# Softmax times values: the values' loads and the ordinary stores move from SyncE's queue to ScalarE's

## The chip, the cores and the metric

The kernel runs on one core of a Trainium2 chip. The metric is the device time in microseconds, the median over several runs. The core's engines are TensorE (PE, with weight loads as PEld), VectorE (DVE), ScalarE (ACT), GpSimd (POOL) and SyncE (SP), which here only issues transfers. A transfer that an engine issues goes into that engine's DMA queue, and 16 DMA engines carry it out.

## The reference

```python
# scores: (8, 12, 1024, 1024) float32, v: (8, 12, 1024, 64) float32
scores_max = np.max(scores, axis=-1, keepdims=True)
attn = np.exp(scores - scores_max)
attn = attn / (np.sum(attn, axis=-1, keepdims=True) + 1e-8)
return np.matmul(attn, v).astype(np.float32)
```

There are 96 heads. Scores are 402.7 MB, values and output 25.2 MB each, so 453 MB cross between HBM and the core's memory.

## The kernel before

The heads are taken four at a time in 24 passes (PASSES), in a hardware loop over m. A pass has two halves, k = 0 and k = 1, of two heads each. Each half has one score buffer s_bufs[k] of 128 partitions by 16 rows (R) by 1024 numbers: a partition holds 16 consecutive rows of one head, 64 KB, and one load(k, m) fills the buffer with 8.39 MB.

For each pair of rows ScalarE takes the exponential into half precision (L425; no maximum is subtracted, and a check at the end of the program turns to a slow general version if numbers leave a safe range). PE transposes (L438), VectorE copies the transposed block out of PSUM (L450, single rows at the end of a pass at L446), and PE multiplies by the values with two columns of ones beside them, which gives the sums of the rows (L160). The product of a row comes three rows (LAG) behind its transposes. VectorE divides (L139, L147) into out_bufs.

The values of a pass, 1.05 MB, are loaded into one tile, v_sb (load_v, L271), in the middle of the pass before. From there POOL spreads them as half precision into vones: spread_v(0) when the last product of k = 0 is done, spread_v(1) at the end of the pass (L283). ScalarE reads them too: watch_v (L295) at the end of a pass checks their range. At the end of a pass POOL also copies the outputs into the tile done (put_by, L178), which is stored in the middle of the next pass by store_before (L191). The last passes differ: the loads for the last two passes come in parts, the outputs of pass 21 wait in done and those of pass 22 in the place of the values (spare), and these and the last pass's own outputs go out through store_last (L202).

All transfers of the loop are issued by SyncE, in an order that is written out: queue(dma) makes each one follow the one before it on that engine. In the middle of pass m load_first (an If at L254) issues the values of pass n = m + 1, the store, and load(0, n); at the end of the pass last (an If at L384, with one at L388 inside) issues load(1, n). A load waits until the exponentials have read the buffer, so load(0, n) waits for the exponentials of k = 0 in pass m. Every load and store of the loop uses one of eight semaphores in turn. Where the two branches of an If use different ones, SyncE makes up for those of the branch not taken at the end of the If, and waits for the transfer that used each of them last.

Of the kernel before, what the change touches and what calls it, by code (L numbers as in the profile page):

```python
# [26 lines left out]
def kernel(  # L27
# [6 lines left out]
    nc = tc.nc  # L34
    P = 128
# [18 lines left out]
    K = AHEAD // T  # L54
    W = P // T
    R = SQ // W
    PASSES = BH // AHEAD
# [2 lines left out]
    GROUPS = -(-R // G)  # L60

    sc_rows = scores.rearrange("b h (j r) k -> (b h j) r k", j=W).rearrange(
        "(m x) r k -> m x r k", x=P
    )
    v_bh = v.rearrange("b h (i t) d -> (b h i) (t d)", i=Q)
    out_rows = out.rearrange("b h (j r) d -> (b h j) (r d)", j=W)
# [21 lines left out]
    done = sb_pool.tile([P, K, R * D], FP32, name="done")  # L88
# [11 lines left out]
    spare = v_sb[:].rearrange("x h s l d -> x (h s l d)").rearrange("x (k y) -> x k y", k=K)  # L100
# [8 lines left out]
    queued = []  # L109
    line = []  # L110

    def after(a, b):

        tc.add_manual_dep(
            a.ins,
            b.ins.name,
            mybir.DependencyInfo(mybir.DependencyClass.NoSync, mybir.DependencyReason.DATA),
            reason="order",
        )
# [7 lines left out]
    def queue(dma):  # L127

        if queued:
            after(dma, queued[-1])  # L130
        queued.append(dma)
# [42 lines left out]
    def put_by(homes):  # L174

        for k in range(K):
            fills.append(
                nc.gpsimd.tensor_copy(  # L178
                    out=homes[:, k], in_=out_bufs[k][:].rearrange("x r d -> x (r d)")
                )  # L180
            )

    def of_pass(m):

        rows = out_rows.rearrange("(m k x) y -> m x k y", k=K, x=P)
        return rows[bass.ds(m, 1)].rearrange("o x k y -> (o x) k y")

    def store_before(m):

        before = (m + (PASSES - 1)) % PASSES  # L190
        send(nc.sync.dma_start(out=of_pass(before), in_=done[:], cond=(before < PASSES - 3)))  # L191

    def send(dma):
        for other in stores:
            apart(dma, other)
            apart(other, dma)
        apart(dma, dma)
        stores.append(dma)
        queue(dma)

    def store_last(to, rows):
        store = nc.sync.dma_start(out=to, in_=rows)  # L202
        ends.append(store)
        send(store)

    def end():

        cut = (GROUPS - 2) * G
        for k, a, b in ((0, 0, R), (1, 0, cut), (1, cut, R)):
            n = BH - AHEAD + T * k  # L210
            store_last(
                out_rows[n * W : (n + T) * W, a * D : b * D],
                out_bufs[k][:, a:b, :].rearrange("x r d -> x (r d)"),
            )
# [4 lines left out]
    def apart(a, b, reason="stores of two heads are disjoint"):  # L219
        tc.declare_no_dep(a.ins, b.ins, across_iterations=True, reason=reason)  # L220
# [16 lines left out]
        users.setdefault((tile.name, bank), []).append(op)  # L237

    def load(k, m, parts=(R,), r=0, **cond):
        rows_n = sc_rows[bass.ds(m * K + k, 1)].rearrange("o x r k -> (o x) r k")  # L240
        for rows in parts:
            queue(
                nc.sync.dma_start(
                    out=s_bufs[k][:, r : r + rows, :], in_=rows_n[:, r : r + rows, :], **cond
                )
            )
            r += rows

    def load_first(m):


        before = queued[-1:]
        n = (m + 1) % PASSES
        with tc.If(m < PASSES - 1) as cmp:  # L254
            load_v(n)
            store_before(m)
            then = queued[-1:]
            with tc.If(m < PASSES - 3) as cmp2:  # L258
                load(0, n)
            with cmp2.Else():  # L260
                queued[:] = then
                load(0, n, (8, 4, 4))
        with cmp.Else():
            queued[:] = before
            store_last(of_pass(PASSES - 3), done[:])
            store_last(of_pass(PASSES - 2), spare)

    def load_v(m, **cond):

        rows = v_bh.rearrange("(m x) y -> m x y", x=P)  # L270
        dma = nc.sync.dma_start(  # L271
            out=v_sb[:].rearrange("x h s l d -> x (h s l d)"),
            in_=rows[bass.ds(m, 1)].rearrange("o x y -> (o x) y"),
            **cond,
        )
        fills.append(dma)
        queue(dma)

    def spread_v(k):

        for t in range(T):
            for s in range(S):
                op = nc.gpsimd.tensor_copy(  # L283
                    out=vones[s * Q : (s + 1) * Q, k, :, t, 0:D].rearrange(
                        "i (h l) d -> i h l d", l=L
                    ),
                    in_=v_sb[(k * T + t) * Q : (k * T + t + 1) * Q, :, s],
                )
        return op

    def watch_v():


        junk = p_bufs[-1][:].rearrange("p r k -> p (r k)")
        return nc.scalar.activation(  # L295
            out=junk,
            in_=v_sb[:].rearrange("p h s l d -> p (h s l d)"),
            func=mybir.ActivationFunctionType.Abs,
            scale=1.0 / SUM_MAX,
            accum_out=seen[:, K * R + 1 : K * R + 2],  # L300
        )
# [8 lines left out]
    def fold():  # L310

        n = K * R + 1
        nc.vector.tensor_reduce(out=seen[:, 0:1], in_=seen[:, 0 : n + 1], axis=X, op=ALU.min)  # L313
        nc.vector.tensor_reduce(  # L314
            out=seen[:, n + 1 : n + 2], in_=seen[:, 1 : n + 2], axis=X, op=ALU.max
        )

    def judge(bank):

        n = K * R + 1  # L320
        part = small("part")
        nc.vector.tensor_scalar(
            out=part, in0=seen[:, n + 1 : n + 2], scalar1=1.0, scalar2=None, op0=ALU.is_le
        )
        nc.vector.scalar_tensor_tensor(  # L325
            out=right, in0=seen[:, 0:1], scalar=1.0 / SUM_MAX, in1=part, op0=ALU.is_ge, op1=ALU.mult
        )
        cell = bank[0:1, G * M : G * M + 1]
        in_line(
            nc.tensor.matmul(  # L330
                out=cell, lhsT=right[:], rhs=vones[:, 0, 0, 0, D : D + 1], start=True, stop=True
            )
        )
        nc.vector.tensor_copy(out=count[:], in_=cell)  # L334
# [45 lines left out]
    def last(m, bank):  # L380

        before = queued[-1:]
        k = K - 1
        with tc.If(m < PASSES - 1) as cmp:  # L384
            spread = spread_v(k)
            watch = watch_v()
            n = (m + 1) % PASSES
            with tc.If(m < PASSES - 3) as cmp2:  # L388
                put_by(done)
                queued[:] = before  # L390
                load(k, n)
            with cmp2.Else():
                with tc.If(m < PASSES - 2) as cmp3:
                    put_by(done)
                with cmp3.Else():
                    gate = nc.gpsimd.tensor_copy(out=cell, in_=out_bufs[k][:, R - 1, D - 1 : D])
                    for op in (watch, spread):
                        tc.add_manual_dep(
                            gate.ins,
                            op.ins.name,  # L400
                            mybir.DependencyInfo(
                                mybir.DependencyClass.Sync, mybir.DependencyReason.DATA
                            ),
                            reason="the values have been read",
                        )
                    put_by(spare)
                queued[:] = before
                load(k, n, (4, 4, 2, 2, 2, 1, 1))
        with cmp.Else():
            queued[:] = before  # L410
            end()
            fold()
            judge(bank)

    def heads(m):

        for k in range(K):
            st = dict(psO=[take(psO_bufs) for g in range(GROUPS)])
            for r in range(R):
# [32 lines left out]
                if r == R - 1 and k < K - 1:  # L452
                    load_first(m)
# [3 lines left out]
        while pending:  # L457
            finish(pending.pop(0))
        last(m, st["psO"][-1])
        for store in ends:  # L460
            for fill in fills:
                apart(fill, store, "no pass comes behind the last stores")

    assert BH % AHEAD == 0 and BH >= 3 * AHEAD and SK == Q * S * C and K == 2
    load_v(0)
    for k in range(K):
        load(k, 0, (R // 2, R // 2) if k == 0 else (R,))
# [44 lines left out]
```

## Time and profile before

| | |
|---|---|
| time, median of 3 runs | 1059.47 us (1059.06 to 1059.63) |
| the profiled execution's own time | 1059.14 us |
| its span in the profile | 1057.4 us |
| mean granted clock of TensorE | 0.89 |
| DMA packets, bytes, mean rate | 19508, 453.06 MB, 428 GB/s |

The profile shows one execution. Busy shares are of the span. In rows of a timeline the first number is the start, the second the length of the stretch, both in us, and a bracket gives the idle time of the engine ahead of it and what ended that. SPq and ACTq are the queues of instructions of SyncE and ScalarE. In rows of DMA queues the columns are packets, MB and the time of the packets as a share of 16 engines over the window. In rows of stages the last three columns are the granted clock, the share of the DMA engines and GB/s.

### The profile page before, as it was taken

The numbers are of one execution on the slowest core, as the hardware profiler recorded it, in microseconds if no ns is written. First come the engines' busy times: TensorE is split into PE (matmuls) and PEld (weight loads), VectorE is DVE, ScalarE is ACT, GpSimd is POOL, SyncE is SP. The second block draws the span as 40 slices with busy tenths as digits, with TensorE's granted clock in tenths as the row PEclk, the third lists the DMA queues.
The fourth block names the chain that finished last, engine by engine and source line by source line (L and its number), as shares of the span: only waits on it lengthen the run. The fifth ranks groups of instructions, "written<-read, shape, count | busy, mean of one in ns | idle before, by whom it ended". The sixth has DMA issues, their size and how long they took to land. (4 is left out here: it accounts for less than half of the span.)

```text
span 1057.4 us, 32323 instructions
## 1 busy us (share of the span) xinstructions
PE 814.7 (77%) x12289; PEld 779.7 (74%) x12289; DVE 705.6 (67%) x1352; ACT 749.6 (71%) x482; POOL 285.5 (27%) x447
## 2 busy tenths in 40 slices
PE   3488678886787868877678877787787876878987
PEld 3487568786787767877668776787777866868887
DVE  2377566675676856767566675676656766667878
ACT  4487578776787667876778667786687856878965
POOL 3041231312412124122241221412224123231241
PEclk9799887898898988889888898898888988988999
DMA  9999999999999999999999999999999999999998
GB/s 397 438 437 421 410 455 426 429 429 425 448 436 436 436 430 440 424 434 431 424 434 434 436 436 436 436 434 414 449 431 434 424 424 441 436 436 420 431 421 322
DMA packets 19508, 453.06 MB, mean 428 GB/s; under 512 B 1840, under 2 KB 1968, under 8 KB 8624
## 3 DMA queue, kind: packets, MB, share of 16 engines
q1 hardware_dynamic: 19504, 452.99, 99.6%
q8 instruction: 4, 0.07, 0.0%
HBM read 427.82 MB, written 27.26 MB: 430 GB/s over the span
## 5 line engine op out<-in xcount | busy, mean ns | idle before, releaser
L425 ACT ACTIVATE p_nat<-s_nat 128x2048 f16<-128x2048 f32 (+1 forms) x432 | 702.4, 1709 | 291.7 <-SPq L388 153.1
L438 PE MATMUL psT<-ident,p_nat 128*128 128x128 f16 x6144 | 521.7, 236 | 213.7 <-ACT p_nat L425 212.3
L450 DVE COPY pt<-psT 128x2048 f16<-128x2048 f16 x336 | 411.3, 1224 | 310.0 <-PE L438 145.0
L438 PEld LDWEIGHTS <-p_nat 128*128 128x128 f16 x6144 | 436.9, 120 | 228.2 <-ACT p_nat L425 224.2
L160 PE MATMUL psO<-vones,pt 128*128 128x130 f16 x6144 | 499.4, 227 | 23.6 <-DVE pt L446 10.8
L283 POOL CAST vones<-v_sb 32x512 f16<-32x512 f32 x392 | 238.1, 607 | 763.6 <-PE L438 388.7
L160 PEld LDWEIGHTS <-pt 128*128 128x128 f16 x6144 | 400.9, 101 | 43.8 <-DVE pt L450 24.9
L147 DVE TENSOR_TENSOR out_sb<-psO,seen 64x192 f32<-64x192 f32 (+1 forms) x576 | 192.0, 333 | 22.1
L446 DVE COPY pt<-psT 128x1024 f16<-128x1024 f16 x96 | 63.4, 681 | 1.5
L139 DVE RECIPROCAL seen<-psO 128x3 f32<-128x3 f32 (+1 forms) x288 | 49.7, 172 | 12.3 <-PE L438 7.1
L295 ACT ACTIVATE p_nat<-v_sb 128x2048 f16<-128x2048 f32 x24 | 45.6, 1900 | 0.7 <-DMA v_sb<-in_v_dram 0.7
L178 POOL COPY done<-out_sb 128x1024 f32<-128x1024 f32 x44 | 44.4, 1035 | 4.7 <-issue 4.7
L295 ACT ACT_TABLE_LOAD x1 | 1.3, 1283 | 5.8 <-DMA v_sb<-in_v_dram 5.8
L313 DVE TENSOR_REDUCE seen<-seen 128x1 f32<-128x34 f32 x25 | 4.7, 189 | 0.8
L295 ACT ACTIVATION_READ_ACCUMULATOR p_nat<-v_sb 128x1 f32 x24 | 4.5, 188 | 0.0
L314 DVE TENSOR_REDUCE seen<-seen 128x1 f32<-128x34 f32 x25 | 4.5, 178 | 0.0
L97 DVE MEMSET done<- 128x1024 f32 x2 | 1.8, 912 | 1.2 <-DVEq L471 1.0
L178 POOL COPY v_sb<-out_sb 128x1024 f32<-128x1024 f32 x2 | 2.0, 1040 | 0.0
L330 PE MATMUL psO<-vones,right 128*1 128x1 f16 x1 | 0.2, 164 | 1.6 <-DVE right L325 1.6
L330 PEld LDWEIGHTS <-right 128*1 128x1 f16 x1 | 0.1, 79 | 1.8 <-DVE right L325 1.8
L334 DVE CAST count<-psO 1x1 int32<-1x1 f32 x1 | 0.1, 145 | 0.3 <-PE psO L330 0.3
masks.py:199 POOL TENSOR_SCALAR_AFFINE_SELECT ident<-ident 128x128 f32<-128x128 f32 x1 | 0.3, 292 | 0.1
(12 smaller groups left out, 1.7 us busy)
## 6 DMA issues: line engine op xcount, KB each, us to landing
v_sb<-in_v_dram SPq DMA_DIRECT2D x24, 1024.0 KB, 17.0
out_dram<-done SPq DMA_DIRECT2D x24, 1024.0 KB, 8.7
s_nat<-in_scores_dram SPq DMA_DIRECT2D x4, 4096.0 KB, 18.7
s_nat<-in_scores_dram SPq DMA_DIRECT2D x8, 2048.0 KB, 25.9
s_nat<-in_scores_dram SPq DMA_DIRECT2D x6, 1024.0 KB, 29.1
s_nat<-in_scores_dram SPq DMA_DIRECT2D x4, 512.0 KB, 26.8
out_dram<-v_sb SPq DMA_DIRECT2D x1, 1024.0 KB
s_nat<-in_scores_dram SPq DMA_DIRECT2D x43, 28.7
```

Of the source, the lines that this page charges most:

```text
L139: nc.vector.reciprocal(out=recip, in_=psO[:, :, D : D + 1])
L147: norm = nc.vector.tensor_tensor(out=out_bufs[k][part, g * G : g * G + rows, :], in0=psO[part, :, t * N : t * N + D], in1=recip[part].to_b ...
L160: product = nc.tensor.matmul(out=st["psO"][g][:, i * M : (i + 1) * M], lhsT=pt[:, c * P : (c + 1) * P], rhs=vones[:, k, c].rearrange("p t ...
L178: nc.gpsimd.tensor_copy(out=homes[:, k], in_=out_bufs[k][:].rearrange("x r d -> x (r d)"))
L283: op = nc.gpsimd.tensor_copy(out=vones[s * Q : (s + 1) * Q, k, :, t, 0:D].rearrange("i (h l) d -> i h l d", l=L), in_=v_sb[(k * T + t) * Q ...
L295: return nc.scalar.activation(out=junk, in_=v_sb[:].rearrange("p h s l d -> p (h s l d)"), func=mybir.ActivationFunctionType.Abs, scale=1. ...
L313: nc.vector.tensor_reduce(out=seen[:, 0:1], in_=seen[:, 0 : n + 1], axis=X, op=ALU.min)
L314: nc.vector.tensor_reduce(out=seen[:, n + 1 : n + 2], in_=seen[:, 1 : n + 2], axis=X, op=ALU.max)
L425: exp = nc.scalar.activation(out=p_nat[:, g : g + rows, :].rearrange("p r (x v) -> p x r v", v=Q * L), in_=s_bufs[k][:, r + g : r + g + ro ...
L438: turned = nc.tensor.transpose(out=psT[:, c * P : (c + 1) * P], in_=p_row[:, c // L, c % L, :], identity=ident16[:],)
L446: copy = nc.vector.tensor_copy(out=pt, in_=psT)
L450: copy = nc.vector.tensor_copy(out=pt2[:], in_=psT2[:])
```

## The change

The values' loads and the ordinary stores (those of passes 0 to 20) are issued by ScalarE; in the middle of a pass the store comes first, then the values. They are no longer in the order that queue keeps for SyncE. The two stores of passes 21 and 22 move from the middle of the last pass to its end, ahead of the last pass's own three, so that SyncE issues the last five stores together. In the last two passes the parts of load(0, n) are 4, 4, 4 and 4 rows instead of 8, 4 and 4, and those of load(1, n) are 4, 2, 2, 2, 2, 2, 1 and 1 instead of 4, 4, 2, 2, 2, 1 and 1. The scores are addressed by (m, k) instead of by m * K + k; the bytes are the same.

```diff
     sc_rows = scores.rearrange("b h (j r) k -> (b h j) r k", j=W).rearrange(
-        "(m x) r k -> m x r k", x=P
+        "(m g x) r k -> m g x r k", g=K, x=P
     )
...
     def store_before(m):
 
         before = (m + (PASSES - 1)) % PASSES
-        send(nc.sync.dma_start(out=of_pass(before), in_=done[:], cond=(before < PASSES - 3)))
+        send(nc.scalar.dma_start(out=of_pass(before), in_=done[:], cond=(before < PASSES - 3)))
...
         stores.append(dma)
-        queue(dma)
 
     def store_last(to, rows):
         store = nc.sync.dma_start(out=to, in_=rows)
         ends.append(store)
         send(store)
+        queue(store)
...
-        rows_n = sc_rows[bass.ds(m * K + k, 1)].rearrange("o x r k -> (o x) r k")
+        rows_n = sc_rows[bass.ds(m, 1), k].rearrange("o x r k -> (o x) r k")
...
         n = (m + 1) % PASSES
-        with tc.If(m < PASSES - 1) as cmp:
+        with tc.If(m < PASSES - 1):
+            store_before(m)
             load_v(n)
-            store_before(m)
-            then = queued[-1:]
             with tc.If(m < PASSES - 3) as cmp2:
                 load(0, n)
             with cmp2.Else():
-                queued[:] = then
-                load(0, n, (8, 4, 4))
-        with cmp.Else():
-            queued[:] = before
-            store_last(of_pass(PASSES - 3), done[:])
-            store_last(of_pass(PASSES - 2), spare)
+                queued[:] = before
+                load(0, n, (4, 4, 4, 4))
 
     def load_v(m, **cond):
 
         rows = v_bh.rearrange("(m x) y -> m x y", x=P)
-        dma = nc.sync.dma_start(
+        dma = nc.scalar.dma_start(
             out=v_sb[:].rearrange("x h s l d -> x (h s l d)"),
...
         fills.append(dma)
-        queue(dma)
...
                 queued[:] = before
-                load(k, n, (4, 4, 2, 2, 2, 1, 1))
+                load(k, n, (4, 2, 2, 2, 2, 2, 1, 1))
         with cmp.Else():
             queued[:] = before
+            store_last(of_pass(PASSES - 3), done[:])
+            store_last(of_pass(PASSES - 2), spare)
             end()
```

## The prediction

> **What bounds the kernel now.** I read the page first: the span, the busy shares, the DMA rows and the queues.
>
> ```profile
> span 1057.4 us, 32323 instructions
> PE 814.7 (77%) x12289; PEld 779.7 (74%) x12289; DVE 705.6 (67%) x1352; ACT 749.6 (71%) x482; POOL 285.5 (27%) x447
> ...
> DMA  9999999999999999999999999999999999999998
> ...
> q1 hardware_dynamic: 19504, 452.99, 99.6%
> ```
>
> No engine is above 77%, but the 16 DMA engines are full in every slice, and all of it is one queue, q1, SyncE's. Then the busy time by stage:
>
> ```profile
> 100.00:940.00 840.00, 655.00 (x9838) 627.11 (x9835) 564.33 (x1082) 595.79 (x385) 226.32 (x348) 0.88 1.00 433
> ```
>
> In the steady part the transfers run at 433 GB/s with a DMA share of 1.00. 452.99 MB at 433 GB/s are 1046 us of the 1057.4. So nothing that frees an engine can help there: the most that any change can win is about 11 us at the two ends, and a change loses wherever it lets the transfers stop. The timelines of SyncE's queue and of ScalarE show a steady pass:
>
> ```profile
> 423.51 0.33 SPq L271 DMA_DIRECT2D v_sb<-in_v_dram  x1
> 424.39 0.41 SPq L191 DMA_DIRECT2D out_dram<-done  x1
> 432.39 19.82 SPq L243 DMA_DIRECT2D s_nat<-in_scores_dram  x2
> ...
> 417.67 14.53 ACT L425 ACTIVATE p_nat<-s_nat 128x2048 f16<-128x2048 f32 x8 [7.61 <-SPq L388]
> 437.03 14.72 ACT L425 ACTIVATE p_nat<-s_nat 128x2048 f16<-128x2048 f32 x10 [4.83 <-DMA s_nat<-in_scores_dram]
> 451.65 1.90 ACT L295 ACTIVATE p_nat<-v_sb 128x2048 f16<-128x2048 f32 x1
> 453.45 0.19 ACT L295 ACTIVATION_READ_ACCUMULATOR p_nat<-v_sb 128x1 f32 x1
> 461.25 9.13 ACT L425 ACTIVATE p_nat<-s_nat 128x2048 f16<-128x2048 f32 x5 [7.61 <-SPq L388]
> ```
>
> A pass is 461.25 - 417.67 = 43.6 us, exactly its 18.87 MB (two score loads of 8.39, values 1.05, store 1.05) at 433 GB/s. ScalarE's exponentials take 14.5 and 14.7 us of it; it waits 7.61 and 4.83 us for scores. The order in the one queue matters: values and store are issued at 423.5 and 424.4, ahead of the next scores (432.4), so they travel between load(1, m), which lands at 437.0, and load(0, n), which lands at 461.2. They are there at about 437.0 + 2.1/0.433 = 441.8. The check of the values (L295) at 451.65 finds them, and then ScalarE waits for scores only. load(0, n) was issued 9.4 us before the engines reach it (441.8 - 432.4): that is the cushion.
>
> **The change, part by part.**
>
> *Store and values on ScalarE's queue.* SyncE loses two issues per pass, ScalarE gains them.
>
> ```profile
> L254 ACTq COMPARE_BRANCH x24: 89/89/107, 46.0 to 1030.7; - x24
> ```
>
> ScalarE comes to that If behind the first exponential of k = 1 (437.0; in pass 0 at 46.0). An issue is 0.33 to 0.41 us, with registers and waits below 1 us each: under 2 us a pass, against 7.61 + 4.83 us of idling. Cost nothing; cover gone, it would be 23 x 2 = 46 us. SyncE issued them at 423.5 and 424.4 behind the same waits (the copies to done, the spread, the last check), 13 us before ScalarE gets there, so no exponential queues behind a wait.
>
> What does cost is where these bytes now stand. At 437 the SyncE queue holds load(0, n), issued at 432.4, and at 452 (14.7 us on) gets load(1, n). The store and the values no longer lie ahead of them but beside them, in another queue of the same 16 engines. How an engine divides itself between two queues the trace can nearly tell. First the size of a step, in the middle of a score load; then a stretch in which another queue had one packet:
>
> ```profile
> q1 hardware_dynamic: 93, 6.09, 100.4%
> ...
> q1 hardware_dynamic: 31, 2.03, 117.9%
> q8 instruction: 1, 0.02, 1.5%
> ```
>
> From 444 to 458 us, 93 packets carry 6.09 MB: 64 KB each, one partition's 16 rows, 1.004 x 16 x 14 / 93 = 2.42 us on an engine. From 26 to 30 us the 8.39 MB load(1, 0) is in flight (8 packets for each engine), and the other queue's 16 KB packet is served inside it, in 1.5% x 64 = 0.96 us. So an engine changes queues between two packets, not at the end of a load. The store is 16 packets of 4 KB per engine, the values 8 of 8 KB (128 x 2 and 128 runs over 16 engines). If engines take turns packet for packet, each of those 24 waits for one of 64 KB. In a pass there are only 16 such packets; so the 16 store packets use up all 16 turns, and the values travel when the score queue is empty: last of all 18.87 MB, 43.6 us after load(0, n) started, not 4.8.
>
> [...] The row above shows a switch inside a load's share, so here one 64 KB run is the unit. [...]
>
> Then the chain of a pass is serial. ScalarE stands at L295 until the values land; behind it in its queue are all exponentials of the next pass, and behind those, by the buffer, load(0, n+1). Idle start of the queue, from the first load:
>
> ```profile
> v_sb<-in_v_dram SPq DMA_DIRECT2D x1, 1024.0 KB, 4.9
> ```
>
> 4.9 us less 2.4 us of transfer leave 2.5 us. Per pass with both loads whole: 2.5 start + 43.6 transfers + 2.1 check (1.90 + 0.19) + 14.5 exponentials of k = 0 = 62.7 us, 19.1 more. It holds for m = 1 to 20: at m = 0 and 22 no store is sent (its cond is false), so the values need 8 turns (8 x 2.7 = 22 us) and cost nothing; at m = 21 the loads are in parts of 16 KB packets (0.6 us) and 24 turns pass in about 19 us. 20 x 19.1 = 382 us. Bounds of the unknown: a start that costs nothing gives 20 x 16.6 = 332. Each turn dearer by what the q8 packet took beyond a quarter of a 64 KB packet (0.96 - 0.61 = 0.35 us) adds 16 x 0.35 x 20 = 112. I take 382: packets follow one another at the full rate in every row, and q8 had a single one.
>
> *Ends.*
>
> ```profile
> SPq L254 <- SPq L254: 3.3, 2, 1.9
> ...
> 1040.42 0.40 SPq L202 DMA_DIRECT2D out_dram<-done  x1
> 1042.84 0.41 SPq L202 DMA_DIRECT2D out_dram<-v_sb  x1
> 1047.11 5.99 SPq L202 DMA_DIRECT2D out_dram<-out_sb  x3
> ...
> 1046.66 1.06 ACT L425 ACTIVATE p_nat<-s_nat 128x1024 f16<-128x1024 f32 x1 [0.45 <-PE psT L438]
> ...
> out_dram<-out_sb SPq DMA_DIRECT2D x1, 128.0 KB, 1.9
> ...
> 1049.30 5.29 POOL L283 CAST vones<-v_sb 32x512 f16<-32x512 f32 x8 [25.64 <-PE psO L160]
> ```
>
> The last row of scores lands at 1046.6; the last store is issued at 1052.77 and lands 1.9 later, 1054.7; POOL's last spread, held back to 1049.3, ends at 1054.6 too. (That spread, eight casts in 5.3 us, starts later in every starved pass as well, but ends under the 14.5 us of the k = 0 exponentials.) At the end of an If, SyncE waits for the loads whose semaphores the branch not taken would have used (the L254 row). Today the stores of passes 21 and 22 are issued ahead of that wait and stand ready in the queue. Changed, they come behind it, at about 1047.1: 2.5 start + 3.15 MB (2.10 + 1.05) / 0.433 = 7.3, so 1056.9 instead of 1054.7: 2.2 us. More parts (4, 4, 4, 4 and 4, 2, 2, 2, 2, 2, 1, 1) move no byte; rows 4 and 5 of the last load land up to 2.4 us earlier, which the stores then cover. Addresses by (m, k) are a matter of SyncE's registers: nothing, since it stands 9.4 us ahead.
>
> **Sum.** Against the profiled execution's own 1059.14 us (span 1057.4 and 1.7 around it; 0.3 below the median 1059.47): 1059.1 + 382 + 2.2 = 1443.3 us.
>
> **Rivals.** *The values come through in time* (0.30). If an engine lets a run of small packets pass in one turn, or divides by bytes, or serves the queues in the order of issue, the values land between 442 and 461. Even at 461 the exponentials of k = 0 start at 463.3, load(0, n+1) is issued at 477.8, and load(1, n) keeps the engines busy until 461.2 + 19.4 = 480.6: no gap. For it: one q8 packet is not a train, and nothing here shows a train. [...] No run here shows two data queues yet. Only the ends count then: 1059.1 + 2.2 = 1061.3, from 1058 to 1064.
>
> *The end gets shorter* (0.08). The same quiet passes, but the rows of the last load decide instead of the stores. The part of 4 rows that becomes 2 + 2 brings rows 4 and 5 2.4 us (1.05 MB) earlier; PE and VectorE, which run behind that burst, end up to 2.4 us earlier; POOL's last spread no longer waits for a store. It decides if the two late stores cost less than their 2.2 us, say because their transfer overlaps the last rows: 1059.1 - 2.4 = 1056.7, faster than before. Against it: 3.15 MB have to leave after 1046.6 in both kernels.
>
> *Partly starved* (0.10). The values get some turns more than one for one, but land late: a gap opens only when they land after 464.0 (480.6 less 2.1 and 14.5), and each us beyond costs 20 us over the 20 passes: 1070 to 1390.
>
> **How the numbers follow.** Turns packet for packet has 0.52: the q8 row gives it the switch between packets, while one for one over a train is not seen. Its own range is 1391 to 1555 (1059.1 + 332; 1443.3 + 112). It is the likeliest, so 1443 is the prediction. The range must reach to the quiet cases: 1057 to 1500 leaves out about 0.05 below and 0.10 above. A measurement of this kernel can tell 0.2% (2.1 us) from no change. Faster by more than that: most of the short end, 0.07. Within it: some two thirds of the quiet rival and the rest of the short end, 0.20. Slower: 0.73, from the turns, the partly starved case and the upper third of the quiet one.
>
> **What would show it.** Right: two hardware queues on the page; values that take about 45 us from issue to landing; the busy tenths of DMA at 6 or 7 in the slices; passes of about 63 us; ScalarE idle before L295 on the values. In the last passes, with parts, values in about 20 us. Wrong: values landing within 20 us of their issue while whole loads run, a DMA share that stays at 1.00, passes of 43.6 us. Then only the end moves: look at the issue of the two stores behind the last scores and at the last landing.

## The result and the profile after

The changed kernel takes 1159.55 us (median of 5 runs, 1156.53 to 1160.56) against 1059.54 us (5 runs beside it): a ratio of 1.0939, 95% interval 1.0927 to 1.0952, 100 us more. The forecast was 1443.

The page of the changed kernel: the span, the busy tenths of the DMA engines, and the queues (packets, MB, share of 16 engines).

```profile
span 1156.6 us, 32596 instructions
DMA  9998998989989899898998989999899898998997
q1 hardware_dynamic: 10912, 405.80, 84.7%
q10 hardware_dynamic: 9168, 47.19, 9.8%
```

There are two hardware queues now, as forecast, but the engines are not idle for a third of the time: 84.7% + 9.8% of 1156.6 us are 1093 us of work and 64 us of idling; before, 99.6% of 1057.4 us were 1053 and 4. So the 99 us between the two spans are some 59 us in which the transfers stop and some 40 us in which the same bytes take longer (the section at the end shows where). The steady part agrees (its last columns are the granted clock, the DMA share and GB/s; before they ended in 1.00 and 433):

```profile
100.00:1000.00 900.00, 611.83 (x9510) 581.06 (x9508) 543.88 (x1041) 581.67 (x374) 223.15 (x342) 0.86 0.95 392
```

ScalarE's timeline over two passes of the changed kernel:

```profile
426.62 1.91 ACT L421 ACTIVATE p_nat<-s_nat 128x2048 f16<-128x2048 f32 x1 [3.23 <-PE psO L160]
427.65 0.42 ACTq L191 DMA_DIRECT2D out_dram<-done  x1
428.35 0.43 ACTq L266 DMA_DIRECT2D v_sb<-in_v_dram  x1
429.14 12.92 ACT L421 ACTIVATE p_nat<-s_nat 128x2048 f16<-128x2048 f32 x9 [0.61 <-PE psT L434]
455.03 1.91 ACT L289 ACTIVATE p_nat<-v_sb 128x2048 f16<-128x2048 f32 x1 [12.96 <-SPq L382]
...
503.41 1.91 ACT L289 ACTIVATE p_nat<-v_sb 128x2048 f16<-128x2048 f32 x1 [12.77 <-SPq L382]
```

A pass is 503.41 - 455.03 = 48.4 us, not 43.6 and not 62.7; times some 21 passes, the 4.8 us are the whole loss. The check of the values (L289 here) waits 13 us, so the values are late, but they are there 26.7 us after their issue (428.35 to 455.03), not 45. (The bracket names SyncE at L382: at the end of that If SyncE waits for the same landing. By the records of the trace the values land at 454.92 and that wait of SyncE ends at 454.96.) How they got through, a view of the DMA queues shows: the packets that started in a window, MB, and their time as a share of 16 engines; first 430 to 446 us, where load(0, n) runs, then 451 to 454 us.

```profile
q1 hardware_dynamic: 96, 6.29, 90.8%
q10 hardware_dynamic: 80, 0.33, 5.0%
...
q10 hardware_dynamic: 208, 1.27, 101.1%
q1 hardware_dynamic: 4, 0.26, 20.1%
```

A run here is one packet of these rows. Up to 446 the forecast's picture holds: 96 runs of 64 KB (6.29 MB) beside 80 of 4 KB (0.33 MB), the store's, 6 and 5 on the average for each of the 16 engines. But from 451 to 454 the engines work almost for q10 alone: the score queue is empty but for the 4 runs that start at the end of the window, and of the rest of the store and the values 208 packets, 1.27 MB, start in these 3 us. What empties it stands in the waits of SyncE's own queue (us in total, times, longest): here of the changed kernel,

```profile
SPq L243 <- DMA s_nat<-in_scores_dram: 906.7, 53, 30.8
```

and here the same line of the kernel before.

```profile
SPq L243 <- DMA s_nat<-in_scores_dram: 81.6, 26, 6.7
```

The issue of a score load waits for the landing of another score load, 17 us on the average, 53 times. In the pass above the timeline of SyncE has load(1, n) at

```profile
451.44 0.34 SPq L243 DMA_DIRECT2D s_nat<-in_scores_dram  x1
```

although ScalarE was through with that buffer at 442 (429.14 + 12.92). load(0, n + 1) follows at 475.35, with the exponentials of k = 0 done at 471.5: neither load waits for ScalarE. The trace's records of the issues tell why: each names the semaphore on which its transfer counts, 110 to 117 for the loop in both traces, counted from 0 below. For the four whole transfers of an ordinary pass they are, in both traces as in the built programs:

| kernel | values | store | load(0, n) | load(1, n) | median, us |
|---|---|---|---|---|---|
| before | 0 | 1 | 2 | 5 | 1059.5 |
| changed | 5 | 4 | 0 | 0 | 1159.6 |

In the changed kernel the two loads of a pass have one semaphore. load(0, n), issued at 426.77, lands 24.4 us later, at 451.14, and load(1, n) is issued at 451.44; that one lands at 475.09, and load(0, n + 1) is issued at 475.35. Of the 46 times that a transfer follows another on semaphore 0 in this trace, none is issued before the landing of the one ahead of it, and 45 within 0.42 us behind it. In the trace of the kernel before load(1, n) is issued at 451.88, ahead of the landing of load(0, n) at 461.15. So the theory for the experiments (A in the expectations): engines do take turns packet for packet, which alone would starve the values; the new numbers of parts put both loads on one semaphore, which alone costs time by stopping the score queue; and in the changed kernel the second ends the starvation that the first would cause.

### The profile page after: what moved, and what is told of

It reads as the page before. It is cut to its first block, busy times and chain, and to the rows that moved or that the text cites. A ratio compares the mean times of both kernels' runs of the same rounds, so it can differ in the third digit from the quotient of the medians.

```text
span 1156.6 us, 32596 instructions
## 1 busy us (share of the span) xinstructions
PE 788.3 (68%) x12289; PEld 749.0 (65%) x12289; DVE 705.3 (61%) x1352; ACT 751.4 (65%) x482; POOL 285.7 (25%) x447
## 3 DMA queue, kind: packets, MB, share of 16 engines
q1 hardware_dynamic: 10912, 405.80, 84.7%
## 5 line engine op out<-in xcount | busy, mean ns | idle before, releaser
L434 PE MATMUL psT<-ident,p_nat 128*128 128x128 f16 x6144 | 505.8, 231 | 326.7 <-ACT p_nat L421 321.6
L434 PEld LDWEIGHTS <-p_nat 128*128 128x128 f16 x6144 | 421.1, 118 | 345.7 <-ACT p_nat L421 338.3
L160 PE MATMUL psO<-vones,pt 128*128 128x130 f16 x6144 | 482.6, 222 | 36.3 <-DVE pt L446 19.2
L160 PEld LDWEIGHTS <-pt 128*128 128x128 f16 x6144 | 385.0, 99 | 56.4 <-DVE pt L446 40.0
L289 ACT ACTIVATE p_nat<-v_sb 128x2048 f16<-128x2048 f32 x24 | 45.8, 1909 | 272.6 <-SPq L382 256.4
L147 DVE TENSOR_TENSOR out_sb<-psO,seen 64x192 f32<-64x192 f32 (+1 forms) x576 | 192.0, 333 | 36.5 <-POOL done L178 16.6
L289 ACT ACTIVATION_READ_ACCUMULATOR p_nat<-v_sb 128x1 f32 x24 | 4.5, 187 | 0.0
```

Of the source, the lines that this page charges most:

```text
L147: norm = nc.vector.tensor_tensor(out=out_bufs[k][part, g * G : g * G + rows, :], in0=psO[part, :, t * N : t * N + D], in1=recip[part].to_b ...
L160: product = nc.tensor.matmul(out=st["psO"][g][:, i * M : (i + 1) * M], lhsT=pt[:, c * P : (c + 1) * P], rhs=vones[:, k, c].rearrange("p t ...
L289: return nc.scalar.activation(out=junk, in_=v_sb[:].rearrange("p h s l d -> p (h s l d)"), func=mybir.ActivationFunctionType.Abs, scale=1. ...
L434: turned = nc.tensor.transpose(out=psT[:, c * P : (c + 1) * P], in_=p_row[:, c // L, c % L, :], identity=ident16[:],)
```

## The experiments

Times are medians; "before" ran beside each and was 1059.5 to 1059.7 throughout. The first four take the parts of the change apart.

**The move alone.** Parts and late stores are as before. (The addressing by (m, k) is in it, as in all kernels here with values and store on ScalarE. It was not tried by itself; the best of these kernels, at 1069.39 us, shows that it is no large term.)

```diff
-        send(nc.sync.dma_start(out=of_pass(before), in_=done[:], cond=(before < PASSES - 3)))
+        send(nc.scalar.dma_start(out=of_pass(before), in_=done[:], cond=(before < PASSES - 3)))
...
+            store_before(m)
             load_v(n)
-            store_before(m)
...
-        dma = nc.sync.dma_start(
+        dma = nc.scalar.dma_start(
```

> Of the change only the move: store and values are issued by ScalarE, store first; parts of the loads and the late stores stay as before. In this kernel the two whole score loads of a pass count on two different semaphores, as in the kernel before, so load(1, n) is in the queue before load(0, n) has landed. Theory A (turns packet for packet, and in the changed kernel an empty score queue that ended the starvation, because there each whole load waits for the landing of the other): with the queue kept full, the values land last, a pass is about 62.7 us, and the time about 1440 us, slower than the changed kernel by about 280. Rival B (the values and store come through beside whole loads; what cost 100 us in the changed kernel is the wait of load for load alone): 1059 to 1064 us. Rival C (moving the transfers is itself the 100 us): about 1160.

Measured: 1226.37 us, ratio 1.1577 (1.1557 to 1.1596). That is between A's 1440 and the rivals' times; ScalarE's timeline says why.

```profile
415.45 1.90 ACT L293 ACTIVATE p_nat<-v_sb 128x2048 f16<-128x2048 f32 x1
...
445.60 0.42 ACTq L191 DMA_DIRECT2D out_dram<-done  x1
446.31 0.36 ACTq L270 DMA_DIRECT2D v_sb<-in_v_dram  x1
...
488.13 1.91 ACT L293 ACTIVATE p_nat<-v_sb 128x2048 f16<-128x2048 f32 x1 [28.18 <-DMA v_sb<-in_v_dram]
...
490.04 12.71 ACT L423 ACTIVATE p_nat<-s_nat 128x2048 f16<-128x2048 f32 x7
501.19 0.42 ACTq L191 DMA_DIRECT2D out_dram<-done  x1
501.88 0.36 ACTq L270 DMA_DIRECT2D v_sb<-in_v_dram  x1
502.65 16.51 ACT L423 ACTIVATE p_nat<-s_nat 128x2048 f16<-128x2048 f32 x11
519.07 1.90 ACT L293 ACTIVATE p_nat<-v_sb 128x2048 f16<-128x2048 f32 x1
```

The pass that ends at 488 is starved: values issued at 446.3 and checked at 488.1, after an idle 28 us. The queues between 450 and 484, 484 and 488, and 501 and 506 us:

```profile
q1 hardware_dynamic: 224, 13.63, 92.5%
q10 hardware_dynamic: 224, 0.92, 6.5%
...
q10 hardware_dynamic: 192, 1.18, 70.2%
...
q10 hardware_dynamic: 306, 1.33, 78.4%
```

224 packets of the one queue and 224 of the other: one for one by the count. The score queue's are 208 runs of 64 KB (13.63 MB) and 16 that move next to nothing; the other 224 are the store's 4 KB (0.92 MB). The values go when the scores are through, 484 to 488. That is the forecast. But the next pass is not starved. Both loads of scores have landed, so ScalarE works without a pause (from 488.13 to 519.07) and its queue runs ahead of it: it issues the store and the values at 501.2 and 501.9, while the last exponential of k = 0 begins only at 502.65. That one, 1.9 us long, releases load(0, n+1), which therefore comes behind, not before 504.5. From 501 to 506 only q10 moves, the values land 6.7 us after their issue, and the check at 519 waits for nothing. Two passes take 519.07 - 415.45 = 103.6 us, 16.4 more than 2 x 43.6; ten pairs make 164 of the 167 us.

**The parts alone**, everything on SyncE.

```diff
-                load(0, n, (8, 4, 4))
+                load(0, n, (4, 4, 4, 4))
...
-                load(k, n, (4, 4, 2, 2, 2, 1, 1))
+                load(k, n, (4, 2, 2, 2, 2, 2, 1, 1))
```

> Of the change only the parts of the last loads (4, 4, 4, 4 and 4, 2, 2, 2, 2, 2, 1, 1); all transfers on SyncE, everything else as before. With these numbers of parts the two whole loads of a pass fall on one semaphore, as in the changed kernel. Theory A: each whole load is issued only when the other has landed, so SyncE's queue runs empty at one of the two loads of a pass (at the other the values and the store fill the start): about 2.5 us a pass, 22 passes, 1110 to 1120 us; long waits of SyncE for score loads in L243. Rival B' (parts that move no byte cost nothing, as I predicted): 1058 to 1060.

Measured: 1149.11 us, ratio 1.0849 (1.0829 to 1.0869). Parts that concern two passes of 24 cost 90 us. A's size was too small: the passes take 47.4 us, not 46.

**The parts one by one.** Only the first of these two lines, and only the second.

> Only the parts of load(0, n) in the last two passes: 4, 4, 4, 4 instead of 8, 4, 4; all transfers on SyncE, no byte moved. With one more transfer in that branch the whole loads load(0, n) and load(1, n) of the ordinary passes come to count on one semaphore. Theory A (the shared semaphore is the 90 us of the kernel with the parts only): 1140 to 1155 us, SyncE waiting some 880 us in L243 for score loads, passes of 47.4 us. Rival F (it is the many small transfers at the end themselves that cost): at most 2 us, 1059 to 1062.

> Only the parts of load(1, n) in the last two passes: 4, 2, 2, 2, 2, 2, 1, 1 instead of 4, 4, 2, 2, 2, 1, 1. Here the whole loads of a pass stay on two different semaphores. Theory A: the ordinary passes are untouched, 43.6 us each, SyncE's wait in L243 for score loads stays near 80 us; 1057 to 1060 us, 0 to 2.4 us faster than before by the earlier rows 4 and 5. Rival F (parts cost as such): half of the 90 us or more.

Measured: 1148.58 us, ratio 1.0840 (1.0823 to 1.0856), for load(0, n); 1059.57 us, ratio 1.0000 (0.9991 to 1.0009), for load(1, n). With the one part more in load(0, n), SyncE's waits and the steady part are

```profile
SPq L243 <- DMA s_nat<-in_scores_dram: 895.8, 50, 33.4
```

```profile
100.00:1000.00 900.00, 648.35 (x9638) 621.41 (x9637) 551.67 (x1054) 586.22 (x378) 220.58 (x337) 0.85 0.95 396
```

as in the changed kernel, with a single queue. The one part more in load(1, n) brings neither a loss nor the gain at the end that a rival of the prediction hoped for.

**The late stores alone, and the change without the move.** The first has only the two late stores at the end; the second has them and the parts; all on SyncE.

```diff
-        with tc.If(m < PASSES - 1) as cmp:
+        with tc.If(m < PASSES - 1):
...
-        with cmp.Else():
-            queued[:] = before
-            store_last(of_pass(PASSES - 3), done[:])
-            store_last(of_pass(PASSES - 2), spare)
...
             queued[:] = before
+            store_last(of_pass(PASSES - 3), done[:])
+            store_last(of_pass(PASSES - 2), spare)
             end()
```

> Of the change only the two late stores: issued by SyncE at the end of the last pass instead of in its middle; all transfers stay on SyncE, parts as before. The two whole loads of a pass count on two semaphores. Theory A and the prediction's tail: passes of 43.6 us, and 2.10 MB more to send after the last scores: 2.2 us more, about 1061.7. Rival I (the stores overlap with the last rows' work): 1059 to 1060.

> The changed kernel without the move: new parts in both loads and the late stores at the end, but store and values on SyncE in the old order. With the branch of the late stores gone, the parts 4, 4, 4, 4 no longer put the two whole loads on one semaphore (load(1, n) shares one with the values' load, which lands 10 us before it is issued). Theory A (the shared semaphore, not the parts, cost the 90 us): passes of 43.6 us, 1059 to 1062 us, against 1148.6 with the parts of load(0, n) alone. Rival F (the parts cost as such): about 1150.

Measured: 1153.62 us, ratio 1.0882 (1.0867 to 1.0897), and 1154.48 us, ratio 1.0893 (1.0878 to 1.0908). Both expectations failed. The values' load and load(1, n) have one semaphore here (the table below); the expectation saw that load(1, n) follows the landing of the values by 10 us, but not that the next values then have to follow load(1, m). The waits of SyncE's queue in the kernel with the late stores alone:

```profile
SPq L267 <- DMA s_nat<-in_scores_dram: 360.0, 22, 17.3
```

and its timeline of SyncE:

```profile
423.82 0.33 SPq L267 DMA_DIRECT2D v_sb<-in_v_dram  x1
424.70 0.41 SPq L191 DMA_DIRECT2D out_dram<-done  x1
425.71 13.26 SPq L243 DMA_DIRECT2D s_nat<-in_scores_dram  x2
```

The values are issued at 423.82, when load(1, m) has landed (ScalarE starts on it at 423.78), and the store and load(0, n) stand behind them: the queue runs empty once a pass, and the share of the DMA engines from 100 to 1000 us is 0.94, not 1.00.

**Two parts more.** Whether parts and late stores cost anything but through the semaphores is told by the last kernel with still more transfers, which happen to give four different semaphores.

```diff
-                load(0, n, (4, 4, 4, 4))
+                load(0, n, (4, 4, 2, 2, 2, 2))
```

> The kernel of the change without the move (154.48 above 1000 us) with two parts more in load(0, n) of the last two passes: 4, 4, 2, 2, 2, 2 instead of 4, 4, 4, 4. More transfers, no byte moved; but with this number the values, the store, load(0, n) and load(1, n) of an ordinary pass count on four different semaphores again, where the kernels with the late stores at the end had the values' load and load(1, n) on one, so that the values' issue waited for load(1, m) to land. Theory A (two of a pass's transfers on one semaphore are the 94 us): passes of 43.6 us, SyncE's waits for score loads in L243 and in the values' line back near 90 us in all; 1059 to 1062 us, of which the late stores at the end are up to 2.2. Rival F (parts and late stores cost as such): 1150 to 1160.

Measured: 1063.07 us, ratio 1.0031 (1.0019 to 1.0043): two more transfers take back 91.4 us. Its waits of SyncE's queue and its steady part:

```profile
SPq L243 <- DMA s_nat<-in_scores_dram: 44.3, 12, 12.0
...
SPq L267 <- DMA s_nat<-in_scores_dram: 12.7, 1, 12.7
```

```profile
100.00:1000.00 900.00, 706.30 (x10644) 676.24 (x10641) 608.49 (x1161) 649.71 (x417) 241.58 (x370) 0.89 1.00 433
```

The steady part is as before, so what is left, 3.4 us, is the end. The semaphores of all the kernels with everything on SyncE:

| kernel | values | store | load(0, n) | load(1, n) | median, us |
|---|---|---|---|---|---|
| parts of load(1, n) | 0 | 1 | 2 | 5 | 1059.6 |
| two more parts | 0 | 1 | 2 | 3 | 1063.1 |
| parts of load(0, n); both parts | 0 | 1 | 2 | 2 | 1148.6; 1149.1 |
| late stores; change without the move | 0 | 1 | 2 | 0 | 1153.6; 1154.5 |

**The changed kernel with its late stores put back** into the middle of the last pass; the loads are on semaphores 0 and 2.

```diff
             load_v(n)
...
+        with cmp.Else():
+            queued[:] = before
+            store_last(of_pass(PASSES - 3), done[:])
+            store_last(of_pass(PASSES - 2), spare)
...
             queued[:] = before
-            store_last(of_pass(PASSES - 3), done[:])
-            store_last(of_pass(PASSES - 2), spare)
             end()
```

> The changed kernel with one thing undone: the two late stores are issued in the middle of the last pass again, in a branch of their own. With them there the two whole loads count on two semaphores again. Theory A: SyncE's queue no longer runs empty, the store takes the turns, and every second pass is starved as in the kernel with the move only: 10 x 16.7 = 167 us, 1215 to 1235 us, so slower than the changed kernel by about 65. Rival G (the place of the late stores only moves the end): 1157 to 1160, less 2.

Measured: 1227.07 us, ratio 1.1577 (1.1559 to 1.1595): undoing a part of the change makes it 67 us slower, as slow as the move alone. With the loads on two semaphores ScalarE's longest wait at the check is 28.6 us, with both on one 13.0: the shared semaphore does protect the changed kernel from the starvation.

The next four vary the order and the size of what takes turns.

**The values first on ScalarE**, in the kernel with the move alone and in the changed one.

```diff
-            store_before(m)
             load_v(n)
+            store_before(m)
```

> As the kernel with the move only, but ScalarE issues the values ahead of the store. Theory A (turns packet for packet): the 8 packets of values per engine need 8 turns beside packets of 64 KB, 8 x 2.6 = 21 us from issue, so they land before load(0, n) does at about 461; no gap opens, and the 16 packets of the store take the next 16 turns, which nothing waits for within the pass: 1059 to 1064 us, DMA share 1.00. Rival D (ScalarE's queue is starved as a whole while score loads are queued, and not by its order): the values still land last, 62.7 us a pass, about 1440. Rival C: about 1160.

> The changed kernel with the values ahead of the store on ScalarE, nothing else. Its two whole loads stay on one semaphore. Theory A: the values now come within 8 turns, but they were through in time in the changed kernel too, when the score queue ran empty; what it loses is the empty queue, which stays: 1150 to 1160 us, about as the changed kernel. Rival E (the changed kernel's 100 us are the wait of ScalarE for the late values): 1059 to 1064 us.

Measured: 1123.44 us, ratio 1.0609 (1.0592 to 1.0627), and 1165.66 us, ratio 1.1005 (1.0987 to 1.1023). The order is worth 103 us to the move alone and nothing to the changed kernel (6 us the other way, not explained). But the first was to be free of loss, and is not. ScalarE's timeline:

```profile
436.85 1.91 ACT L293 ACTIVATE p_nat<-v_sb 128x2048 f16<-128x2048 f32 x1 [10.31 <-PE psO L160]
...
453.44 1.91 ACT L423 ACTIVATE p_nat<-s_nat 128x2048 f16<-128x2048 f32 x1 [0.16 <-DMA s_nat<-in_scores_dram]
457.21 0.35 ACTq L270 DMA_DIRECT2D v_sb<-in_v_dram  x1
...
483.18 1.91 ACT L293 ACTIVATE p_nat<-v_sb 128x2048 f16<-128x2048 f32 x1 [11.02 <-PE psO L160]
```

A loop closes through ScalarE: 16.6 us from the check over the exponentials of k = 0, 3.8 to the issue, 26.0 from there to the next check, 46.3 in all (the profile puts the wait down to PE; the values' median from issue to landing is 25.4 us, so it is these). The 3.8 us show what the new order does to the store. Of POOL's timeline:

```profile
455.05 2.02 POOL L178 COPY done<-out_sb 128x1024 f32<-128x1024 f32 x2 [7.54 <-DMA out_dram<-done]
```

The store now lands last, at 455.05; POOL's copy into done waits 7.5 us for it, and the values are issued when the copy ends, at 457.2. So the store is waited for within a pass too. The expectation had weighed the landing of the values only against the end of the transfers, not against this loop, and had said that nothing waits for the store.

**Score loads in runs of 16 KB**, with the move alone; then the same with the values first.

```diff
-                    out=s_bufs[k][:, r : r + rows, :], in_=rows_n[:, r : r + rows, :], **cond
+                    out=s_bufs[k][:, r : r + rows, :], in_=rows_n[:, r : r + rows, :],
+                    max_dma_last_dim=16384, **cond
```

> As the kernel with the move only (store first, then values, on ScalarE; two semaphores), but the score loads are cut into runs of 16 KB instead of 64 KB, the same bytes. Theory A (one run of each queue in turn): 16 turns of 0.61 + 0.16 us and 8 of 0.61 + 0.31 us are 12.3 + 7.4 = 19.7 us instead of 39 and more, so the values land some 25 us after the issue, at about 462, and no pass is starved; the runs themselves take 4 x 611 = 2444 ns instead of 2418 per 64 KB, 1.1% or 11 us: 1065 to 1085 us. Rival H (the score queue goes first whatever the size of its runs, or the engine shares by bytes): starved as before, about 1226 to 1240.

> As the kernel with the move, values ahead of the store, and score loads in runs of 16 KB. Theory A with a loop through ScalarE (issue of the values, their turns, the check, eight exponentials, the next issue): in the kernel with small runs and the store first this loop is 2.1 + 14.5 + 3.0 + 1.7 + 25.4 = 46.7 us; the values first need 8 turns of 0.92 = 7.4 us instead of 19.7, so the loop falls to some 34 us and the transfers bound a pass again: 43.6 x 1.011 = 44.1, 1068 to 1076 us in all. Rival J (two data queues at once cost rate as such): about 1099 again.

Measured: 1099.42 us, ratio 1.0380 (1.0364 to 1.0396), and 1069.39 us, ratio 1.0092 (1.0077 to 1.0108). With the store first, the queues from 456 to 464 us:

```profile
q1 hardware_dynamic: 162, 2.65, 77.5%
q10 hardware_dynamic: 170, 0.70, 21.1%
```

Still about one for one (162 and 170), but a turn is now 16 KB (2.65 MB in 162 packets), and the check follows the values' issue by 25.5 us, not by 41.8 as in the starved pass of the move alone: the starvation is gone. The loop through ScalarE is left, in the timeline of the same kernel:

```profile
430.23 1.91 ACT L294 ACTIVATE p_nat<-v_sb 128x2048 f16<-128x2048 f32 x1 [11.11 <-DMA v_sb<-in_v_dram]
...
449.62 1.91 ACT L424 ACTIVATE p_nat<-s_nat 128x2048 f16<-128x2048 f32 x1 [2.97 <-PE L160]
...
451.34 0.36 ACTq L271 DMA_DIRECT2D v_sb<-in_v_dram  x1
...
476.81 1.91 ACT L294 ACTIVATE p_nat<-v_sb 128x2048 f16<-128x2048 f32 x1 [11.83 <-DMA v_sb<-in_v_dram]
```

476.81 - 430.23 = 46.6 us, 25.5 of it from the values' issue to the check; the expectation had missed the loop. With the values first as well, the issues' row (KB each, median us from issue to landing) and the steady part are

```profile
v_sb<-in_v_dram ACTq DMA_DIRECT2D x24, 1024.0 KB, 11.8
```

```profile
100.00:1000.00 900.00, 702.16 (x10574) 670.67 (x10572) 604.68 (x1154) 645.93 (x414) 246.45 (x378) 0.89 1.01 431
```

The values need 11.8 us; by that the loop would be some 33 us (46.6 less 25.4 and 11.8 more), an estimate, and the transfers bound the pass again, with two queues at work all the time. Of the 9.75 us that remain against before, some 4 are the steady part (431 GB/s against 433; the store of pass 21 is issued at 1044.41 instead of 1040.42). The expectation had put 1.1%, 11 us, on the 16 KB runs. The other 6 us come at the end. In the last but one pass ScalarE stands idle for 12 us, by the profile until a store lands:

```profile
1009.25 12.91 ACT L424 ACTIVATE p_nat<-s_nat 128x2048 f16<-128x2048 f32 x9 [11.96 <-DMA out_dram<-done]
```

and its last exponential ends at 1053.1 instead of 1047.7. No kernel of the study beats the one before.

## Why the prediction was wrong, and where it was right

**Right: the bound and the turns.** With a DMA share in the steady part of 1.00 the kernel takes 1059 us, with 0.95 (the changed kernel) 1160, with 0.87 (the move alone) 1226: what stopped the transfers cost time. While load(0, n) and load(1, n) run, as many packets of the one queue go as of the other, 224 and 224 from 450 to 484 us of the move alone; there the store uses up the turns of the scores and the values go last. The rival that the values come through in time (1061.3) is refuted for loads in runs of 64 KB (1226.37 with the move alone): only with small runs and the values first does the time come near it (1069.39).

Issuing from ScalarE saved nothing here: the same transfers, moved there, cost 167 us by themselves, and still 10 once the values go first and the runs are small.

**Wrong, the step that failed: "more parts move no byte", cost nothing.** With it fell "at 452 (14.7 us on) gets load(1, n)". The parts of load(0, n) alone cost 89 us, because they change which transfers share a semaphore; with the late stores it is another pair and 94. In the changed kernel load(1, n) is not issued while load(0, n) is in flight (it is issued at 451.44, behind the landing at 451.14), so the score queue beside store and values runs empty after the 128 runs of one load, not the 256 of two. From 428 to 448 us 96 packets of q10, all of 4 KB, went beside it; the rest of the store and the values came from 450 on, when it ended, and the 62.7 us pass never comes about. The prediction quoted the wait at the end of an If for semaphores of the branch not taken, and priced it for the last pass only; that the numbers themselves move (load(1, n) from 5 to 2 with one part more in load(0, n)) was not looked at.

**Wrong too, though hidden by the first: "it holds for m = 1 to 20".** Even with the loads apart only every second pass starves, since after a starved pass ScalarE's queue issues the store and the values ahead of load(0, n+1) (501.2 and 501.9 in the move alone, the load not before 504.5). That would have been 1226, not 1443; the price of a starved pass, 19.1, measured 16.4 for the pair.

**Right by accident: the direction and the range.** The changed kernel is slower because its two loads share a semaphore, not because the values starve; that both go the same way is luck. The partly starved case had the time between its ends, but not this mechanism: in it the values still came through by turns.

**The end.** The forecast was 2.2 us for the late stores; with the semaphores apart the end costs 3.4 (1063.07 against 1059.62). The last five stores are issued together by SyncE there. The first and the last of them, and the row of the last (its last number is the time from issue to landing), are

```profile
1047.04 0.41 SPq L202 DMA_DIRECT2D out_dram<-done  x1
...
1051.82 0.33 SPq L202 DMA_DIRECT2D out_dram<-out_sb  x1
...
out_dram<-out_sb SPq DMA_DIRECT2D x1, 128.0 KB, 4.5
```

The first is the forecast's 1047.1. The last lands at 1056.3, 1.6 us later than the 1054.7 before and 0.6 earlier than the forecast's 1056.9. The other 1.8 us lie behind that landing and stay open.

**The sum by measured terms.** Late stores and parts with semaphores apart, 3.4; a pair of a pass's transfers on one semaphore, 91.4 (1154.48 - 1063.07); the move on top of that, 5.1 (1159.55 - 1154.48): 99.9 of 100.0. The pair is not the same in the last two kernels, so the 5.1 is a difference of two bounds and not a price of the move; it holds the addressing as well. By itself the move costs 167.

## What to carry to other kernels

Here one part more in a branch of the last two passes moved load(1, n) of every ordinary pass from semaphore 5 to 2, that of load(0, n), and cost 89 us; two parts more in another kernel took 91 back. After such an edit, read which of the steady loop's transfers share one, and look in the issuing queue's own waits for an issue that waits for a landing. Before small transfers are moved to a second queue beside one that is always full, count the turns: in the move alone 224 small runs went beside 224 packets of the big queue. Put what is waited for first (1226.37 to 1123.44 here), look for what waits for the transfer that now comes last (here POOL's copy, 7.5 us for the store), and make the big runs smaller if that isn't enough (1123.44 to 1069.39). Two faults can hide each other: with both, this kernel takes 1159.55 us, with the move alone 1226.37, so undoing one part at a time would have misled.

## What the hardware showed unexpectedly

Two queues at work together cost next to no rate in the kernel with values first and runs of 16 KB: 431 GB/s in the steady part against 433. But in the changed kernel some runs of load(0, n) take longer. Two windows of 2 us, 446 to 448 with the last 16 runs of load(0, n), and 476 to 478 with the first 16 of load(0, n + 1), and one of 2.5 us, 453 to 455.5, with the first 16 of load(1, n):

```profile
q1 hardware_dynamic: 16, 1.05, 183.1%
...
q1 hardware_dynamic: 16, 1.05, 158.0%
...
q1 hardware_dynamic: 16, 1.05, 102.7%
```

16 runs of 64 KB, as many as there are engines, take 1.831 x 2 = 3.66 us and 3.16 us each on the average, against 2.42 in the middle of a load (456 to 472 us: 110 runs, 103.9%). The 1.24 and 0.74 us more, in 21 passes, are 42 us, about the 40 us of longer transfers. The empty score queue alone is not the reason: load(1, n) starts behind one too, and its first 16 runs take 1.027 x 2.5 = 2.57 us on the average. Why the runs at the two ends of load(0, n) are slow was not tried.

And in the kernel with the move alone ScalarE's queue issued the store at 501.19, before the engine was through with the work ahead of it: an exponential that stands ahead of the store starts at 502.65. That decided in every second pass who came first.
